# Attention layer of an encoder trunk: ScalarE in written order in the q, k, v stage, and VectorE in place of accumulating DMAs in the output projection

## The chip, the cores and the metric

The kernel runs on one core of a Trainium2 chip. The metric is the device time of one execution in microseconds, as the median of several executions. The engines of the core have names in the profile: PE is TensorE (matmuls; PEld its weight loads), DVE is VectorE, ACT is ScalarE, POOL is GpSimd and SP is SyncE, which issues most of the DMAs.

## The reference

Two layers over two sequences of 512 tokens with 1024 features: a Fourier mixer with its MLP, then grouped-query attention with its MLP. All values are fp32. The change lies in the attention layer:

```python
def gqa_attention(h, w_qkv, q_gain, k_gain, w_o):
    B, S, _ = h.shape
    qkv = h @ w_qkv
    ...
    q = rms_norm(q, q_gain)
    k = rms_norm(k, k_gain)
    ang_row, ang_col = axial_angles(S)
    q = axial_rope(q, ang_row, ang_col) * (HEAD_DIM ** -0.5)
    k = axial_rope(k, ang_row, ang_col)
    ...
        s = jnp.einsum("bqkgd,bskd->bkgqs", q_blk, k)
        p = jax.nn.softmax(s, axis=-1)
        return jnp.einsum("bkgqs,bskd->bqkgd", p.astype(v.dtype), v)
    ...
    return o @ w_o

def trunk(...):
    for i in range(DEPTH):
        ...
            x = x + gqa_attention(rms_norm(x, attn_norm[j]), ...)
        x = x + sq_relu_mlp(rms_norm(x, mlp_norm[i]), mlp_w_up[i], mlp_w_down[i])
    return rms_norm(x, final_norm)
```

There are 8 heads of 128 features and 2 key and value heads, so 16 heads in all over both sequences.

## The kernel before

**Numbers.** Every fp32 operand is split into a high and a low half in a rounded format: ScalarE casts the high half (`split`, L85) and VectorE subtracts it for the low one (L86). A product is three matmuls (`mm3`, L80 to L82; `product`, L835). The large products with weights use sums of blocks in the manner of Strassen and Winograd, so that four blocks need seven products; `Blocks` makes these sums of the activations, and the weights' own sums come from `keep` and other helpers.

**Stages around the change.** `second_product(0)` ends the first MLP; its adds of PSUM into the result are L1039, its last ones with the common part L1179 and L1180. Then come three column groups, `cg` = 2 (k and v), 0 and 1 (q), in that order; for each group two sequences, and for each of these four tiles of 128 tokens. One tile is 24 matmuls into one of eight PSUM banks (`qkv`). ScalarE copies the tile to SBUF with the token's scale (L1506, L1511), squares each head with a sum (`head_squares`, L1325), and `norm_rope` takes the root (L134 to L140: VectorE, with the square root L135 on ScalarE), scales the heads by it (ScalarE, L1343), and rotates (VectorE L1348 and L1351, GpSimd L1353). `norm_rope` is a generator: its first part runs with its own tile, the rest one tile later. In between a step of `keep` is taken, which loads rows of the weight `w_o`, forms their block sums on VectorE (L1441), splits them (L1459) and stores them in DRAM (`kept`).

**The transition.** The last two tiles of q are worked in among the first heads. Between them stand head 0's scores (`scores`: maximum L1385 on VectorE, exponential L1387 on ScalarE, reciprocal L1388, scaling L1389 on GpSimd) and head 1's transposed q (`transpose_q`: L1374 on TensorE, then a split).

**Heads.** In step n TensorE does, four times over, a block of scores of head n and four transposes of the probabilities of head n−1 (L1395), then L1374 for head n+1 and the 12 matmuls of the values of head n−1 (`values`). In steps 6, 8, 10 and 12 `load_kept` (L1551) loads one of the first rows of `w_o` and splits it in two halves.

**Output projection** (from L1554). Its seven products are turned over four row blocks `m`: first b11 and b21, which give the first sequence's first half, then t2, t3, t4, then t1 and b22. The product of b11 plus that of t2 is a common part `e[m]`, to which three of the four result blocks add. `add` (L1561) is VectorE's add of a PSUM bank, and `common` (L1565) starts DMAs on GpSimd's queue that add `e[m]` to a block of the result. Each finished block is squared (`square`: L160 on ScalarE, sums L164 on GpSimd, or left apart for the last), multiplied by its gain (L206) and stored (`put_away`). The squares are summed over features by L172 on TensorE; from these come the root and its spread over the tokens (L180), and with them the operands of the second MLP (L219 norm, L235 `first_lo`).

**What sets the order.** Each engine runs its own queue in order. The order of a queue is mostly made by a scheduler at build time; within `manual_schedule` an engine's instructions stand in the order in which the code is written. Buffers come from pools: `u` (activations), `t` (temporaries), `w` (weights), `raw` (landed weights) and `ps` (the eight PSUM banks).

Of the kernel before, what the change touches and what calls it, by code (L numbers as in the profile page):

```python
# [18 lines left out]
P = 128  # L19
# [24 lines left out]
def trunk_kernel(ctx, tc, x_in, xt_in, y_out, dcos, dsin, feat, rope, gfour, gcol, grow, gfin,  # L44
# [1276 lines left out]

    def head_squares(raw, h0, n, ss):
        junk = tm((P, n * HD), BF16)
        for h in range(h0, h0 + n):
            nc.scalar.activation(junk[:, (h - h0) * HD : (h - h0 + 1) * HD], raw[:, h * HD : (h + 1) * HD],  # L1325
                                 AF.Square, accum_out=ss[:, h : h + 1])

    def norm_rope(raw, nh, table, ts, outs, ss=None, step=None, eng=nc.vector):

        n = nh * len(ts)  # L1330
        step = nh if step is None else step
        if ss is None:
            ss = small(n)
            head_squares(raw, 0, n, ss)
        r = small(n)
        rsqrt(r[:, :n], ss[:, :n], n, 1.0 / HD)
        yield
        for h0 in range(0, n, step):
            t = ts[h0 // nh]
            t1, t2 = [tm((P, step, HD)) for _ in range(2)]  # L1340
            x = raw[:, h0 * HD : (h0 + step) * HD].rearrange("p (h d) -> p h d", h=step)
            for i in range(step):
                nc.scalar.activation(x[:, i], x[:, i], AF.Copy, scale=r[:, h0 + i : h0 + i + 1])  # L1343
# [118 lines left out]
    def load_kept():  # L1462

        i = len(ahead)
        if i < 4:
            w = load_w(w_o[i, 0], nc.vector, 2)
        elif i in (8, 9):
            w = load_w(w_a22[i - 8])
        else:
# [4 lines left out]
            w = t[:, 0], t[:, 1]  # L1474
        ahead.append([(w[0][:, i : i + 512], w[1][:, i : i + 512]) for i in (0, 512)])

# [5 lines left out]
    keeping, turned = keep(), iter(())  # L1482
    for cg in (2, 0, 1):
        ws = wkv if cg == 2 else [load_w(w_qkv[cg, u], home=own if u < 2 else lent) for u in range(4)]
        for q in range(NSEQ):
            if cg == 2:
                vt[q] = (slot([P, NT, 256], F32R), slot([P, NT, 256], F32R))
                kr[q] = slot([P, NT, 256], F32)
            else:
                for i in range(2):  # L1490
                    qr[q, 2 * cg + i] = slot([P, NT, 256], F32)
            for t in range(NT if (cg, q) != (1, 1) else 2):
                if (cg, q, t) in transposes:
                    transpose_k(transposes[cg, q, t])
                if (cg, q, t) == (1, 1, 1):
                    first = transpose_q(0, 0)
                if (cg, q) == (2, 0):
                    o = qkv(cg, q, t, ws, KC - 2, KC, begun[t])
                else:
                    o = qkv(cg, q, t, ws)  # L1500
                if (cg, q, t) == (2, 0, 0):
                    token_scale(1)
                r = rs[q][:, t : t + 1]
                if cg == 2:
                    raw = tm((P, 256))
                    nc.scalar.activation(raw, o[:, :256], AF.Copy, scale=r)  # L1506
                    split_scaled(vt[q][0][:, t], vt[q][1][:, t], o[:, 256:], r)
                    todo = norm_rope(raw, NKV, rt["k"], [t], [kr[q][:, t]])
                else:
                    raw = slot([P, 512], F32) if (cg, q, t) == (1, 1, 1) else tm()  # L1510
                    nc.scalar.activation(raw, o, AF.Copy, scale=r)  # L1511
                    todo = norm_rope(raw, 4, rt["q"], [t], [qr[q, 2 * cg + i][:, t] for i in range(2)])
                next(todo)
                for _ in turned:
                    pass
                turned = todo
                if cg != 2 or q or t:
                    next(keeping, None)


    heads = [(q, h) for q in range(NSEQ) for h in range(NH)]
    raw, ss = slot([P, 1024], F32), small(8)
    o = qkv(1, 1, 2, ws)
    probs = [scores(*heads[0], first, t) for t in range(NT)]
    nc.scalar.activation(raw[:, :512], o, AF.Copy, scale=rs[1][:, 2:3])
    head_squares(raw, 0, 4, ss)
    qT = transpose_q(*heads[1])
    for _ in turned:
        pass
    o = qkv(1, 1, 3, ws)  # L1530
    nc.scalar.activation(raw[:, 512:], o, AF.Copy, scale=rs[1][:, 3:4])
    todo = norm_rope(raw, 4, rt["q"], [2, 3], [qr[1, 2 + i][:, t] for t in (2, 3) for i in range(2)],
                     ss, 2, nc.gpsimd)
    assert next(keeping, 0) == 0
    for n in range(1, len(heads) + 1):
        pts, nxt = [], []
# [23 lines left out]
    def add(x, o):  # L1560
        nc.vector.tensor_add(x, o, x)  # L1561

    def common(m, *xs):
        for x in xs:
            nc.gpsimd.dma_start(x, e[m], accum_op=ALU.add)  # L1565

# [8 lines left out]
    with tc.manual_schedule(engines={ET.PE}):  # L1575
        o = {}
        for m, i in turn():
# [3 lines left out]
            if i:  # L1581
                add(xs[0, m][:, 0], o[m])
                load_kept()
            else:
                nc.scalar.copy(e[m], o[m])
            if m + i > 1:
                next(todo)
        load_xs(1, park[1])
        for k, name in enumerate(("t2", "t3", "t4")):
            h = heads_out.operand(name)  # L1590
            for m in range(4):
                o = ps()
                product(o, ahead[4 + 2 * k + m // 2][m % 2], h)
# [8 lines left out]
                if k == 2:  # L1602
                    blocks.gain(0, 2 * m)
                    blocks.gain(0, 2 * m + 1)
                    put_away(0, m)
                if m % 2:
                    load_kept()
                next(todo, None)
        o = {}
        for j, (m, i) in enumerate(turn()):  # L1610
# [13 lines left out]
            if 1 < j < 6:  # L1624
                blocks.first(j - 2)
            if 2 < j < 7:
                blocks.first_lo(j - 3)
    second_product(1, blocks, ())
    ats = []
# [269 lines left out]
```

## Time and profile before

| | |
|---|---|
| median of 3 runs | 1716.38 us (1715.95 to 1716.51) |
| the profiled execution | 1714.8 us |
| its span, first to last instruction | 1713.0 us |
| mean granted TensorE clock | 0.994 |
| q, k, v stage, transition, heads, projection | from about 740, 850, 870, 992 us of the span |

In the page's first part stand each engine's busy time, its share of the span and its number of instructions. A row of a timeline has the start in us from the span's begin, the duration, the engine, the line, the operation, its buffers (out<-in), its shape and the number of instructions that were joined to one row; behind it in brackets how long the engine had been idle and what ended this. A row of groups has busy time, the mean in ns of one instruction and the idle time before them with what ended it. A row of windows has the length, then PE, PEld, DVE, ACT and POOL with busy time and count, then the granted clock, the busy share of the DMA engines and GB/s.

### The profile page before, as it was taken

The numbers are of one execution on the slowest core, as the hardware profiler recorded it, in microseconds if no ns is written. First come the engines' busy times: TensorE is split into PE (matmuls) and PEld (weight loads), VectorE is DVE, ScalarE is ACT, GpSimd is POOL, SyncE is SP. The second block draws the span as 40 slices with busy tenths as digits, with TensorE's granted clock in tenths as the row PEclk, the third lists the DMA queues.
The fourth block names the chain that finished last, engine by engine and source line by source line (L and its number), as shares of the span: only waits on it lengthen the run. The fifth ranks groups of instructions, "written<-read, shape, count | busy, mean of one in ns | idle before, by whom it ended". The sixth has DMA issues, their size and how long they took to land.

```text
span 1713.0 us, 22359 instructions
## 1 busy us (share of the span) xinstructions
PE 1666.6 (97%) x7826; PEld 1386.3 (81%) x7826; DVE 1260.9 (74%) x1880; ACT 885.6 (52%) x1568; POOL 384.1 (22%) x360
## 2 busy tenths in 40 slices
PE   5999999999999999999989999999999999999998
PEld 4988888888888888788868887788788888888887
DVE  8769777546886869977678773787855577878875
ACT  6766445446342434456788753564444563433334
POOL 1320443231000001333344323102432220000002
PEclk9999999999999999999999999999999999999999
DMA  8652555449864757435400158334543596756622
GB/s 276 164 206 98 189 186 185 166 168 339 292 221 154 244 179 224 158 139 181 142 25 1 50 179 239 141 110 156 201 168 142 199 373 212 240 157 218 186 105 99
DMA packets 123394, 304.54 MB, mean 178 GB/s; under 512 B 12537, under 2 KB 13689, under 8 KB 123281
## 3 DMA queue, kind: packets, MB, share of 16 engines
q1 hardware_dynamic: 99040, 254.61, 42.1%
q0 software_dynamic: 9984, 22.55, 6.6%
q10 hardware_dynamic: 14256, 25.96, 4.0%
q8 instruction: 61, 1.00, 0.2%
q14 instruction: 53, 0.43, 0.1%
HBM read 216.49 MB, written 82.38 MB: 174 GB/s over the span
## 4 chain that ended last, share of the span: by engine, by line
PE 42%; DVE 4%; ACT 3%; DMA 1%; issue 1%; POOL 0%; DVEq 0%; ACTq 0%; POOLq 0%
PE ps L835 34%; PE ps L81 2%; PE ps L82 2%; PE ps L80 2%; PE ps L1395 1%; DMA raw<-w_sum 1%; DVE u L86 1%; ACT t L1325 1%; DMA u<-t 0%; ACT t L1387 0%; ACT t L1343 0%; ACT u L85 0%; DVE w L86 0%; PE ps L172 0%; PE ps L1374 0%
## 5 line engine op out<-in xcount | busy, mean ns | idle before, releaser
L835 PE MATMUL ps<-u,w 128*128 128x512 f32 x4992 | 1145.2, 390 | 5.0 <-DVE w L86 2.9
L835 PEld LDWEIGHTS ps<-u,w 128*128 128x128 f32 x4992 | 936.6, 188 | 204.3 <-DVE w L86 4.7
L85 ACT CAST w<-raw 128x1024 fp32r<-128x1024 f32 (+1 forms) x226 | 220.2, 981 | 318.3 <-PE ps L835 244.8
L86 DVE TENSOR_TENSOR w<-raw,w 128x1024 fp32r<-128x1024 f32 (+1 forms) x226 | 262.5, 1166 | 82.5 <-ACT w L85 82.2
L85 ACT CAST u<-u 128x1024 fp32r<-128x1024 f32 x144 | 144.6, 1047 | 82.2 <-PE ps L835 38.9
L86 DVE TENSOR_TENSOR u<-u,u 128x1024 fp32r<-128x1024 f32 x144 | 173.3, 1231 | 16.2 <-ACT u L85 15.8
L80 PE MATMUL ps<-u,u 128*128 128x512 f32 (+2 forms) x360 | 137.1, 383 | 7.0 <-ACT u L85 3.7
L1039 DVE TENSOR_TENSOR u<-ps,u 128x512 f32<-128x512 f32 x160 | 109.3, 684 | 36.6 <-PE ps L835 34.0
L949 POOL TENSOR_TENSOR u<-u 128x512 f32<-128x512 f32 x28 | 37.7, 1347 | 430.4 <-ACT u L848 430.4
L835 PE MATMUL ps<-u,u 128*128 128x512 f32 x552 | 132.2, 390 | 2.0 <-DVE t L918 2.0
L1068 POOL DMA_DIRECT2D raw<-w_sum x32 | 27.9, 871 | 471.2 <-DMA raw<-w_sum 158.7
L82 PE MATMUL ps<-u,u 128*128 128x512 f32 (+2 forms) x360 | 132.4, 368 | 1.0 <-DVE u L86 0.6
L81 PE MATMUL ps<-u,u 128*128 128x512 f32 (+2 forms) x360 | 131.6, 366 | 0.3 <-DVE u L86 0.3
L835 PEld LDWEIGHTS ps<-u,u 128*128 128x128 f32 x552 | 103.4, 188 | 24.5 <-issue 2.8
L164 POOL TENSOR_TENSOR t<-t,t 128x512 f32<-128x512 f32 (+1 forms) x52 | 76.8, 1481 | 169.5 <-ACT t L160 168.8
L847 ACT ACTIVATE t<-t 128x512 f32<-128x512 f32 x64 | 40.4, 632 | 114.1 <-DVE t L918 104.3
L80 PEld LDWEIGHTS ps<-u,u 128*128 128x128 f32 x360 | 69.8, 194 | 17.5 <-ACT u L85 4.4
L82 PEld LDWEIGHTS ps<-u,u 128*128 128x128 f32 x360 | 69.6, 193 | 12.5 <-DVE u L86 1.6
L81 PEld LDWEIGHTS ps<-u,u 128*128 128x128 f32 x360 | 70.0, 194 | 8.8 <-DVE u L86 0.9
L86 DVE TENSOR_TENSOR u<-ps,u 128x512 fp32r<-128x512 f32 (+4 forms) x118 | 70.7, 623 | 8.1 <-ACT u L85 7.7
L907 DVE TENSOR_TENSOR t<-ps,u 128x512 f32<-128x512 f32 x32 | 22.0, 687 | 62.0 <-PE ps L835 58.3
L160 ACT ACTIVATE t<-u 128x512 f32<-128x512 f32 (+1 forms) x64 | 37.8, 603 | 56.9 <-DVE u L1561 29.9
(236 smaller groups left out, 1993.0 us busy)
## 6 DMA issues: line engine op xcount, KB each, us to landing
raw<-w_up SPq DMA_DIRECT2D x80, 512.0 KB, 4.5
u<-spill_t SPq DMA_DIRECT2D x60, 512.0 KB, 7.1
raw<-w_sum SPq DMA_DIRECT2D x56, 512.0 KB, 5.3
u<-spill_b SPq DMA_DIRECT2D x45, 512.0 KB, 6.3
spill_t<-u SPq DMA_DIRECT2D x84, 256.0 KB, 2.0
spill_b<-t ACTq DMA_DIRECT2D x60, 256.0 KB, 4.2
raw<-w_row SPq DMA_DIRECT2D x28, 512.0 KB, 4.4
park<-u SPq DMA_DIRECT2D x24, 512.0 KB, 4.3
```

The costliest lines, as they stand in the source:

```text
L80: nc.tensor.matmul(out, lh, rh, start=first, stop=False)
L81: nc.tensor.matmul(out, lh, rl, start=False, stop=False)
L82: nc.tensor.matmul(out, ll, rh, start=False, stop=last)
L85: nc.scalar.copy(dst_hi, src)
L86: eng.tensor_sub(dst_lo, src, f32(dst_hi))
L160: nc.scalar.activation(s[:, :n], xt(q, fo)[:, :n], AF.Square)
L164: nc.gpsimd.tensor_add(acc[q][:, :n], acc[q][:, :n], s[:, :n])
L835: nc.tensor.matmul(o, w[x][:, sl], h[k][y], start=first and k + i == 0, stop=k == n - 1 and i == 2, skip_group_check=not first)
L847: nc.scalar.activation(t, src, AF.Relu)
L949: eng.tensor_sub(t[:, 0], b12, b11)
L1039: nc.vector.tensor_add(x, o, x)
L1068: nc.gpsimd.dma_start(s[:, 1], w[:, 3], accum_op=ALU.add)
```

## The change

It has three parts.

*q, k, v.* `tile_qkv` no longer copies a tile out of PSUM. The squares read the PSUM bank with the token's scale r, the root is multiplied by r (one small VectorE operation more per tile), and the scaling before the rotation reads PSUM too and writes a temporary; the bank is held until the next tile. Only the last three tiles are still copied. ScalarE's instructions stand in written order in the three groups and in the transition. The weights of the next group are loaded and split one per tile (`next_ws`), and `keep` starts at the second sequence of group 2.

*First rows.* `load_kept` is a generator: in steps 7 and later of the heads' loop it loads a first row of `w_o` into an activation buffer and splits one half per step, in steps 8 to 15. Before, the scheduler had drawn these splits forward into the q, k, v stage and the transition (w<-raw of 128x512 there).

*Output projection.* `common` is gone. At t2 VectorE adds the bank to `e[m]` and `e[m]` to the first sequence's second half; at t3 it adds the bank and then `e[m]` to both halves of the second sequence in one instruction 1024 wide; t4 accumulates in the PSUM bank of t3. The squares of the first sequence's even blocks move from t3 to t2, and their gains from t4 to t3. `first_lo` of blocks 2 and 3 is written after the loop.

```diff
-    def norm_rope(raw, nh, table, ts, outs, ss=None, step=None, eng=nc.vector):
+    def norm_rope(raw, nh, table, ts, outs, ss=None, step=None, eng=nc.vector, scale=None):
...
-            head_squares(raw, 0, n, ss)
+            head_squares(raw, 0, n, ss, 1.0 if scale is None else scale)
+            yield
         r = small(n)
         rsqrt(r[:, :n], ss[:, :n], n, 1.0 / HD)
+        if scale is not None:
+            nc.vector.tensor_scalar(r[:, :n], r[:, :n], scale, 1.0, ALU.mult, ALU.mult)
         yield
...
-            x = raw[:, h0 * HD : (h0 + step) * HD].rearrange("p (h d) -> p h d", h=step)
+            y = raw[:, h0 * HD : (h0 + step) * HD].rearrange("p (h d) -> p h d", h=step)
+            x = y if scale is None else tm((P, step, HD))
             for i in range(step):
-                nc.scalar.activation(x[:, i], x[:, i], AF.Copy, scale=r[:, h0 + i : h0 + i + 1])
+                nc.scalar.activation(x[:, i], y[:, i], AF.Copy, scale=r[:, h0 + i : h0 + i + 1])
...
-            w = load_w(w_o[i, 0], nc.vector, 2)
+            raw, w = slot([P, 1024], F32), own()
+            nc.sync.dma_start(raw, w_o[i, 0])
...
+        for j in range(2 if i < 4 else 0):
+            yield
+            split(*ahead[i][j], raw[:, j * 512 : j * 512 + 512])
...
+    def tile_qkv(cg, q, t):
...
+        r = rs[q][:, t : t + 1]
+        if cg == 2:
+            split_scaled(vt[q][0][:, t], vt[q][1][:, t], o[:, 256:], r)
+            return norm_rope(o, NKV, rt["k"], [t], [kr[q][:, t]], scale=r)
+        outs = [qr[q, 2 * cg + i][:, t] for i in range(2)]
+        if (cg, q, t) != (1, 1, 1):
+            return norm_rope(o, 4, rt["q"], [t], outs, scale=r)
+        raw = slot([P, 512], F32)
+        nc.scalar.activation(raw, o, AF.Copy, scale=r)
+        return norm_rope(raw, 4, rt["q"], [t], outs)
...
+    with tc.manual_schedule(engines={ET.Activation}):
+        for cg in (2, 0, 1):
+            later = next_ws({2: 0, 0: 1}[cg]) if cg != 1 else iter(())
...
+                    todo = tile_qkv(cg, q, t)
+                    next(todo)
+                    for _ in turned:
+                        pass
+                    if q or t > 1 or cg == 0:
+                        next(later, None)
+                    for _ in range(cg != 2 or q):
+                        next(keeping, None)
+                    next(todo)
+                    turned = todo
...
-        if n in (6, 8, 10, 12):
-            load_kept()
+        if n > 6:
+            next(first_rows, None)
...
-    def common(m, *xs):
-        for x in xs:
-            nc.gpsimd.dma_start(x, e[m], accum_op=ALU.add)
...
-                if k < 2:
-                    add(e[m], o)
-                    common(m, *((xs[1, m][:, 0],), (xs[0, m][:, 1], xs[1, m][:, 1]))[k])
+                    o[m] = ps()
+                product(o[m], ahead[4 + 2 * k + m // 2][m % 2], h, k < 2)
+                if k == 0:
+                    add(e[m], o[m])
+                    square(0, 2 * m)
+                    add(xs[0, m][:, 1], e[m])
+                elif k == 1:
+                    add(xs[1, m][:, 1], o[m])
+                    add(xs[1, m], e[m].unsqueeze(1).broadcast_to([P, 2, 512]))
+                    blocks.gain(0, 2 * m)
                 else:
-                    add(xs[0, m][:, 1], o)
-                if k:
-                    fo = 2 * m + k - 1
-                    square(0, fo, alone=fo == KC - 1)
...
+                    add(xs[0, m][:, 1], o[m])
+                    square(0, 2 * m + 1, alone=m == 3)
```

How the rows stand now. ScalarE at the transition, before: the tile (1,1,1) of q is copied (L1511), squared and scaled (L1343), tile (1,1,2) copied (L1525); then the exponentials' table and head 0's exponentials (L1387), and the cast of head 1's transposed q (L85).

```order
L1511 ACTIVATE u_7623<-ps_7598,rs_6317 128x512
L1325 ACTIVATE t_7626,s_7625<-u_7623 128x128 x4
L135 ACTIVATE s_7634<-s_7632 128x4
L1343 ACTIVATE u_7623<-u_7623,s_7631 128x128 x4
L1525 ACTIVATE u_7654<-ps_7656,rs_6317 128x512
L1387 ACT_TABLE_LOAD
L1387 ACTIVATE t_7688,s_7686<-ps_7681,s_7685 128x512
L1387 ACTIVATE t_7699,s_7697<-ps_7692,s_7696 128x512
L85 CAST u_7736<-ps_7731 128x512
```

The same place with the change (lines moved by 5 and more: L1528 and L1563 are the copies, L1348 the scaling, L1392 the exponentials):

```order
L1528 ACTIVATE u_7624<-ps_7599,rs_6319 128x512
L1325 ACTIVATE t_7627,s_7626<-u_7624 128x128 x4
L1348 ACTIVATE t_7634<-ps_7530,s_7578 128x128 x4
L135 ACTIVATE s_7647<-s_7645 128x4
L1392 ACT_TABLE_LOAD
L1392 ACTIVATE t_7693,s_7691<-ps_7686,s_7690 128x512
L1392 ACTIVATE t_7704,s_7702<-ps_7697,s_7701 128x512
L1392 ACTIVATE t_7715,s_7713<-ps_7708,s_7712 128x512
L1392 ACTIVATE t_7726,s_7724<-ps_7719,s_7723 128x512
L1563 ACTIVATE u_7657<-ps_7661,rs_6319 128x512
L85 CAST u_7736<-ps_7731 128x512
```

Between squares and root of tile (1,1,1) now stands the scaling of the tile before it (t_7634 from PSUM); its own scaling has gone behind the cast, and four exponentials instead of two stand ahead of the cast.

VectorE in the projection from t3 on, before (t_9394 to t_9397 are `e`, u_9398 to u_9404 the first sequence's blocks, u_9559 one of the second's):

```order
L86 TENSOR_TENSOR u_9673<-u_9345,u_9672 128x1024
L1561 TENSOR_TENSOR t_9395<-ps_9676,t_9395 128x512
L1561 TENSOR_TENSOR t_9396<-ps_9698,t_9396 128x512
L1561 TENSOR_TENSOR t_9397<-ps_9717,t_9397 128x512
L1561 TENSOR_TENSOR u_9398<-ps_9739,u_9398 128x512
L1561 TENSOR_TENSOR u_9400<-ps_9760,u_9400 128x512
L1561 TENSOR_TENSOR u_9402<-ps_9784,u_9402 128x512
```

With the change (L1599 is `add`; t_9400 to t_9403 are `e`, u_9565 to u_9571 the second sequence, u_9404 the first):

```order
L86 TENSOR_TENSOR u_9689<-u_9349,u_9688 128x1024
L1599 TENSOR_TENSOR u_9565<-t_9400,u_9565 128x1024
L1599 TENSOR_TENSOR u_9567<-ps_9692,u_9567 128x512
L1599 TENSOR_TENSOR u_9569<-ps_9712,u_9569 128x512
L1599 TENSOR_TENSOR u_9567<-t_9401,u_9567 128x1024
L1599 TENSOR_TENSOR u_9569<-t_9402,u_9569 128x1024
L1599 TENSOR_TENSOR u_9571<-ps_9729,u_9571 128x512
L1599 TENSOR_TENSOR u_9571<-t_9403,u_9571 128x1024
L1599 TENSOR_TENSOR u_9404<-ps_9671,u_9404 128x512
```

The adds of a bank to `e` at t3 have become adds to the second sequence, and behind each stands an add of `e`, 1024 wide, with both inputs in SBUF.

VectorE at the end of the first MLP, before: the adds of `keep` (L1441) stand among those of the product (L1039).

```order
L1180 TENSOR_TENSOR u_4162<-u_4162,t_3889 128x1024
L1039 TENSOR_TENSOR u_3824<-ps_5997,u_3824 128x512
L1441 TENSOR_TENSOR raw_6386<-raw_6386 128x512
L90 SCALAR_TENSOR_TENSOR u_5961<-u_4044,gc,u_5961 128x512
L1179 TENSOR_TENSOR u_3824<-u_3824,t_3889 128x512
L1039 TENSOR_TENSOR u_4277<-ps_6094,u_4277 128x512
L1441 TENSOR_TENSOR raw_6386<-raw_6386,raw_6387 128x512
L1441 TENSOR_TENSOR raw_6592<-raw_6592,raw_6591 128x512
L1441 TENSOR_TENSOR raw_6387<-raw_6387,raw_6386 128x512
L1039 TENSOR_TENSOR u_4277<-ps_6108,u_4277 128x512
```

With the change:

```order
L1180 TENSOR_TENSOR u_4162<-u_4162,t_3889 128x1024
L86 TENSOR_TENSOR w_6060<-raw_5995,w_6060 128x1024
L1039 TENSOR_TENSOR u_3824<-ps_5997,u_3824 128x512
L1179 TENSOR_TENSOR u_3824<-u_3824,t_3889 128x512
L90 SCALAR_TENSOR_TENSOR u_5961<-u_4044,gc,u_5961 128x512
L1039 TENSOR_TENSOR u_4277<-ps_6094,u_4277 128x512
L1039 TENSOR_TENSOR u_4277<-ps_6108,u_4277 128x512
```

The adds of `keep` are gone from there, and L1180 stands ahead of a weight's split (L86), which it followed before.

More of the change, by code (lines that the diff above doesn't have):

```diff
@@ new lines, in trunk_kernel, with next_ws, split_ws @@
+    ws = {2: wkv}
+    def next_ws(cg):
+        ws[cg], raw = [], []
+        for u in range(4):
+            raw.append(load_raw(w_qkv[cg, u]))
+            if u:
+                yield
+                split_ws(cg, raw[u - 1])
+        yield
+        split_ws(cg, raw[3])
+        yield
+    def split_ws(cg, raw):
+        w = (own if len(ws[cg]) < 2 else lent)()
+        split(*w, raw)
+        ws[cg].append(w)
+    def tile_qkv(cg, q, t):
+        if (cg, q, t) in transposes:
+            transpose_k(transposes[cg, q, t])
+        if (cg, q) == (2, 0):
+            o = qkv(cg, q, t, ws[cg], KC - 2, KC, begun[t])
+        else:
+            o = qkv(cg, q, t, ws[cg])
+        if (cg, q, t) == (2, 0, 0):
+            token_scale(1)
+        r = rs[q][:, t : t + 1]
[8 more added lines that the diff above has]
+        return norm_rope(raw, 4, rt["q"], [t], outs)
@@ L1521, in trunk_kernel @@
     heads = [(q, h) for q in range(NSEQ) for h in range(NH)]
     raw, ss = slot([P, 1024], F32), small(8)
[L1523 to L1531, printed above, removed]
+    with tc.manual_schedule(engines={ET.Activation}):
+        o = qkv(1, 1, 2, ws[1])
+        probs = [scores(*heads[0], first, t) for t in range(NT)]
+        nc.scalar.activation(raw[:, :512], o, AF.Copy, scale=rs[1][:, 2:3])
+        qT = transpose_q(*heads[1])
+        for _ in turned:
+            pass
+        o = qkv(1, 1, 3, ws[1])
+        nc.scalar.activation(raw[:, 512:], o, AF.Copy, scale=rs[1][:, 3:4])
+        head_squares(raw, 0, 4, ss)
@@ L1625, in trunk_kernel @@
                 blocks.first(j - 2)
-            if 2 < j < 7:
+            if 2 < j < 5:
                 blocks.first_lo(j - 3)
+        for i in range(2, 4):
+            blocks.first_lo(i)
     second_product(1, blocks, ())
```

64 lines of the change are left out of this document (19 added, 45 removed).

## The prediction

> **What bounds the kernel now.** First the page's busy times, then TensorE's timeline at every place where it idles, then what ScalarE (ACT) and VectorE (DVE) did just before. All sums are against the profiled execution, 1714.8 us (span 1713.0 and 1.8 around it); the median shown, 1716.4, is 1.6 above it.
>
> ```profile
> PE 1666.6 (97%) x7826; PEld 1386.3 (81%) x7826; DVE 1260.9 (74%) x1880; ACT 885.6 (52%) x1568; POOL 384.1 (22%) x360
> ```
>
> TensorE (PE) is busy for 97%: the matmuls, which the change leaves as they are, are the bound. What can be won is idle time and half-clock time after it. Four such places lie near the edit. The transition from projection to heads, TensorE's timeline (start, us, what, idle before):
>
> ```profile
> 854.12 0.60 PE L1374 MATMUL ps<-ident,u 128*128 128x128 f32 x4
> 854.47 0.49 PE L80 MATMUL ps<-w,u 128*128 128x512 f32 x1
> ...
> 859.83 0.39 PE L82 MATMUL ps<-u,u 128*128 128x512 f32 x1
> 863.42 0.50 PE L80 MATMUL ps<-u,u 128*128 128x512 f32 x1 [3.21 <-ACT u L85]
> ...
> 867.20 0.47 PE L1395 MATMUL ps<-ident,t 128*128 128x128 f32 x1 [1.54 <-POOL t L1389]
> ...
> 872.73 0.60 PE L1374 MATMUL ps<-ident,u 128*128 128x128 f32 x4
> 880.47 0.60 PE L1374 MATMUL ps<-ident,u 128*128 128x128 f32 x4
> ```
>
> From 854.47 to 859.83 stand 24 matmuls, 0.233 apart, so work could have gone on at 860.06. A head takes 7.74 (872.73 to 880.47); less 0.35 for L1374 and 12 matmuls (2.8) the four blocks of scores and transposes are 4.6. L1374 was therefore due at 864.7 and came at 872.73: **8.0 lost**, of it 3.21 and 1.54 in waits and the rest at half clock. The windows, whose third number from the end is the granted clock before DMA share and GB/s:
>
> ```profile
> 864.60:871.40 6.80, 5.26 (x18) 3.82 (x18) 6.80 (x12) 5.66 (x18) 4.35 (x5) 0.50 0.26 82
> 1052.30:1059.20 6.90, 6.75 (x23) 5.97 (x24) 0.72 (x5) 2.20 (x6) 0.00 (x0) 0.51 0.87 308
> 1083.00:1090.00 7.00, 7.00 (x31) 5.66 (x32) 3.71 (x3) 1.92 (x4) 0.93 (x1) 1.00 0.58 195
> ```
>
> Two stretches of about 6.8 us run at 0.50, behind the two longest waits; no other stretch here does. The second is the end of the output projection's first half:
>
> ```profile
> 1050.77 0.38 PE L172 MATMUL ps<-ones,t 128*128 128x2 f32 x2 [2.02 <-POOL t L164]
> 1052.45 3.15 PE L172 MATMUL ps<-ones,t 128*128 128x2 f32 x14 [1.30 <-ACT t L160]
> 1055.46 7.46 PE L835 MATMUL ps<-u,w 128*128 128x512 f32 x24
> 1062.76 0.60 PE L180 MATMUL ps<-ident,s 128*128 128x128 f32 x4
> 1063.12 0.71 PE L835 MATMUL ps<-u,w 128*128 128x512 f32 x2
> ...
> 1099.00 0.95 PE L172 MATMUL ps<-ones,t 128*128 128x2 f32 x8
> ```
>
> TensorE had run dry at 1048.75 (1050.77 less 2.02). At full clock, eight L172 take 0.95: sixteen 1.9, the 24 matmuls 5.6, L180 0.36 (1062.76 to 1063.12), so the last row was due near 1056.5: **6.6 lost**.
>
> **The change part by part.** *Transition.* ScalarE before it, and its groups from 747 to 860 (busy, mean ns, idle before):
>
> ```profile
> 854.41 0.66 ACT L1511 ACTIVATE u<-ps,rs 128x512 f32<-128x512 f32 x1
> 858.28 1.28 ACT L1343 ACTIVATE u<-u,s 128x128 f32<-128x128 f32 x4 [1.15 <-DVE s L140]
> 859.47 0.67 ACT L1525 ACTIVATE u<-ps,rs 128x512 f32<-128x512 f32 x1
> 860.16 1.28 ACT L1387 ACT_TABLE_LOAD   x1
> 862.79 0.58 ACT L85 CAST u<-ps 128x512 fp32r<-128x512 f32 x1
> ```
> ```profile
> L1343 ACT ACTIVATE t<-t,s 128x128 f32<-128x128 f32 x68 | 23.1, 392 | 20.1 <-DVE s L140 20.0
> L1325 ACT ACTIVATE t<-t 128x128 bf16<-128x128 f32 x68 | 20.2, 300 | 0.3
> L1459 ACT CAST t<-raw 128x512 fp32r<-128x512 f32 x16 | 9.7, 609 | 0.0
> L85 ACT CAST w<-raw 128x512 fp32r<-128x512 f32 (+1 forms) x7 | 5.5, 806 | 2.2 <-DMA raw<-w_qkv 1.3 <-DMA raw<-w_o 0.9
> ```
>
> ScalarE is late there because each tile's L1343 waits 1.15 for VectorE's root; the idle sum of 20 us is this wait. Tile (1,1,1) left TensorE about 24 matmuls and a score block (8.4) before 854.1, and is copied only at 854.41. In the new order the previous tile's rotation fills the wait, the copies are gone, and the cast of head 1's q stands behind four exponentials and one copy. Scores of head 0 end on TensorE near 854.1. The last exponential then ends near 856.0 (two take 862.79 − 861.44, so 0.68 each, after VectorE's maximum of about as long), the copy adds 0.67, the cast 0.58: 857.3, the low half 0.7 later. TensorE wants it at 860.06, so 2 us to spare. GpSimd's scalings, which cost the 1.54, follow the exponentials and come earlier too. What is late next: four squares (4 × 0.30) now stand ahead of head 1's first exponential. That can cost nothing or, where nothing covers it, 1.2; I take 0.3, near nothing, since that head's probabilities are transposed a whole head later. **−7.7.**
>
> The clock's part of this is read from the windows. The Trainium skill ("TensorE: Matmul & The Clock Gate", Part 1: The HAM clock gate) has the clock halve after one idle window of about 3.4 us and return after one busy window; by that each half-clock stretch would cost 1.7, not 3.1 to 3.3, and the sum an estimated 3 less. The windows show 6.8 us each, and a drop behind 2.02 + 1.30 with matmuls between, so the measurement decides and the sum goes by the rows.
>
> *Projection.* VectorE at the stall, and GpSimd's accumulating transfers (count, min/median/max ns):
>
> ```profile
> 1037.90 0.69 DVE L1561 TENSOR_TENSOR u<-ps,u 128x512 f32<-128x512 f32 x1 [2.03 <-PE ps L835]
> ...
> 1045.62 0.69 DVE L1561 TENSOR_TENSOR u<-ps,u 128x512 f32<-128x512 f32 x1 [4.30 <-DMA u<-t]
> 1051.05 1.29 DVE L1561 TENSOR_TENSOR u<-ps,u 128x512 f32<-128x512 f32 x2 [4.74 <-DMA u<-t]
> ```
> ```profile
> L1565 POOL DMA_DIRECT2D u<-t x12: 855/872/1197, 1017.3 to 1045.8; - x12
> DMA to landing us min/median/max: 3.9/7.5/9.3
> ```
>
> The last adds wait 4.30 and 4.74 for transfers that land up to 9.3 us after issue; the squares and L172 follow. The change drops these twelve issues (12 × 0.87 of GpSimd, off the path) and gives VectorE eight more adds. Their price, same engine, 1012 to 1110:
>
> ```profile
> L235 DVE TENSOR_TENSOR u<-u,u 128x1024 fp32r<-128x1024 f32 x4 | 7.5, 1889 | 0.0
> L86 DVE TENSOR_TENSOR u<-u,u 128x1024 fp32r<-128x1024 f32 x5 | 6.0, 1217 | 0.0
> ```
>
> Four are 1024 wide, four half that: 4 × 1.22 + 4 × 0.69 = 7.6, or at most 4 × 1.89 + 4 × 0.95 = 11.4. From the end of one tile near 1013.4 to the last near 1046.1 pass 12 tiles of 2.72 (0.69 + 2.03), 32.7 us; VectorE has 12 adds (8.3), eight splits at 1.22 (9.8) and these 7.6: 25.7. The lag it builds up in t2 and t3 is given back in t4, where each tile leaves 2.03. The last add then ends at 1046.8, the last square 0.63 later (it stands alone on ScalarE), and TensorE wants it at 1048.6: no wait, no half clock. **−6.6**; at the upper price 29.5, still inside.
>
> A rule speaks against this: by the Trainium skill ("SBUF — State Buffer", Who interferes with whom) a VectorE instruction with two inputs in SBUF contends with a GpSimd instruction that reads SBUF. The trace agrees (1889 against 1217 ns for one shape); it is the upper price, and a rival below.
>
> *End of the first MLP.* TensorE, then VectorE:
>
> ```profile
> 710.39 8.00 PE L835 MATMUL ps<-u,w 128*128 128x512 f32 x34 [1.07 <-DVE w L86]
> 719.20 2.14 PE L835 MATMUL ps<-u,w 128*128 128x512 f32 x8 [0.81 <-DVE u L1039]
> ```
> ```profile
> 710.25 1.21 DVE L1180 TENSOR_TENSOR u<-u,t 128x1024 f32<-128x1024 f32 x1
> ...
> 714.46 4.09 DVE L1441 TENSOR_TENSOR raw<-raw,raw 128x512 f32<-128x512 f32 x3
> ```
>
> keep() starts later, so its three adds (4.09) no longer stand before L1039: −1.1 (0.81 and the pipeline's refill). In its place L1180 (1.21) instead of an add of 0.68 stands ahead of the split that TensorE awaits at 710.39: +0.5. **−0.6**, between −1.1 and +0.5, if the first goes by another wait.
>
> *First rows among the heads.* Eight splits of 512, one in each of heads 8 to 15, which hold none now:
>
> ```profile
> 866.28 1.14 ACT L85 CAST w<-raw 128x512 fp32r<-128x512 f32 x2
> 867.34 1.82 DVE L86 TENSOR_TENSOR w<-raw,w 128x512 fp32r<-128x512 f32 x2
> 925.00:960.00 35.00, 35.00 (x201) 29.30 (x200) 28.18 (x62) 27.69 (x66) 12.48 (x19) 1.00 0.00 1
> ```
>
> A head of 7.74 leaves ScalarE 1.6 and VectorE 1.5; a split takes 0.57 and 0.91. So between nothing and 8 × 1.48 = 11.8 (no cover at all); I take +0.4, near nothing, because both fit. **Sum: −7.7 − 6.6 − 0.6 + 0.4 = −14.5**: 1700.3 of the profiled run, 1701.9 beside the median.
>
> **Rivals.** (1) *The transition's wait only moves*: four exponentials instead of two stand before the cast; were ScalarE still 5 us behind, nothing there is won: 1709.6. Against it: the wait that made the lag is filled. (2) *VectorE bounds the projection*: with every two-input operation at the 1889 price (adds 11.4, splits 15.1, PSUM adds 8.3: 34.8 of 32.7) the last add is 2.1 late, past a slack of 1.2; with a clock drop 3.3 + 0.9 return, at worst all 6.6: 1706 to 1708.5. Against it: GpSimd has less to do there than before. (3) *The heads lose* the whole uncovered price: 1713.3. (4) **Slower**: ScalarE's written order blocks. Every cast of keep (L1459) and of weights now stands in line before the squares that release PSUM; if the data come late, all wait. A tile lasts 5.6; ScalarE needs 1.2 + 1.6 + 0.61 + 0.2 + at most 1.05, 4.7, so 0.9 is free. Over 16 tiles the transfers would have to hold it 1.8 per tile (14.5 / 16 and the 0.9) to eat the whole gain and reach 1716.4, and 2.0 to pass 0.2%, about 1720. Its casts waited 2.2 for transfers in the whole stage. (5) *first_lo moved to after the loop*: VectorE's order there is unchanged, so the stalls behind it stay; nothing in the sum rests on it.
>
> **Chances.** Forecast 0.72; (1) 0.09; (2) 0.08; (3) or a good part of it 0.05; (4) 0.03; a sum short for reasons not seen 0.03. The range goes from 1698.5 (nothing given back in the transition, the heads or the MLP's end: 1700.7; the gap of 1.6 between profile and median gone; the 0.6 over which the runs spread) to 1710, which takes in (1) and (2). Faster by over 0.2%, about what a measurement can tell from no change (below 1713): 0.92; within: 0.04; slower: 0.04.
>
> **What would show it.** Right: no clock at 0.5 between 860 and 1060 of the old time, L1374 18.6 us apart become 10.7, L172 without idle before it, no accumulating transfer, heads 8 to 15 at 7.74. Wrong: L80 waiting for ACT L85 again, VectorE's adds without idle in t4, a head at 8 or more with the weight cast ahead, TensorE idle behind ScalarE's squares between 747 and 850.

## The result and the profile after

The changed kernel takes 1707.38 us (median of 4 runs, 1705.45 to 1708.37) against 1716.16 for the kernel before in the same sessions: the ratio is 0.9948, with an interval of 0.993 to 0.9965. Of the 14.5 us that the prediction summed up, 8.8 came. The changed kernel's profiled execution was the slowest of its four (1708.37, span 1706.6), so the two profiles differ by 6.4 only. The sums below are between profiled executions.

Where the time went is read from TensorE's starts at five places that every version has: the first L172 behind the first MLP, the first transposes of q (L1374 before, L1379 after), those of head 3, those of the last head, and the add of the projection that waits 0.7 (1075.01 before, 1069.38 after). Differences of these starts, in us:

| stretch | before | after | predicted change | measured change |
|---|---|---|---|---|
| to the first L172 | 738.41 | 738.90 | −0.6 | +0.5 |
| q, k, v, to the first transposes of q | 101.61 | 101.54 | 0 | −0.1 |
| transition, to head 3's transposes | 40.45 | 39.95 | −7.7 | **−0.5** |
| heads, to the last one's transposes | 95.55 | 96.56 | +0.4 | +1.0 |
| projection, to the add that waits 0.7 | 98.99 | 92.43 | −6.6 | **−6.6** |
| rest of the span | 637.99 | 637.22 | 0 | −0.8 |

The projection did what was worked out; the transition did not. First the projection. TensorE's timeline of the changed kernel at the place where it had idled 2.02 and 1.30:

```profile
1049.85 1.84 PE L172 MATMUL ps<-ones,t 128*128 128x2 f32 x16
1051.55 5.75 PE L835 MATMUL ps<-u,w 128*128 128x512 f32 x24
1057.13 0.60 PE L180 MATMUL ps<-ident,s 128*128 128x128 f32 x4
```

No row has a wait in brackets, and the 24 matmuls take 5.75 instead of 7.46. VectorE ahead of it, from the last tiles of t3 on:

```profile
1033.61 1.28 DVE L1599 TENSOR_TENSOR u<-ps,u 128x512 f32<-128x512 f32 x2
1034.81 2.35 DVE L1599 TENSOR_TENSOR u<-t,u 128x1024 f32<-128x1024 f32 x2
1037.08 0.69 DVE L1599 TENSOR_TENSOR u<-ps,u 128x512 f32<-128x512 f32 x1
1037.80 1.23 DVE L1599 TENSOR_TENSOR u<-t,u 128x1024 f32<-128x1024 f32 x1
1039.16 0.69 DVE L1599 TENSOR_TENSOR u<-ps,u 128x512 f32<-128x512 f32 x1
1041.88 0.69 DVE L1599 TENSOR_TENSOR u<-ps,u 128x512 f32<-128x512 f32 x1 [2.03 <-PE ps L835]
```

VectorE falls behind in t3 (it is hardly idle from 1033.6 to 1039.2), and from t4's second tile on it waits 2.03 for TensorE again: the lag is given back where the prediction put it. The wide add costs 1.23 or less, the lower price.

Now the transition. TensorE's timeline of the changed kernel:

```profile
855.95 0.79 PE L80 MATMUL ps<-u,u 128*128 128x512 f32 x1 [3.98 <-ACT u L85]
...
861.54 0.72 PE L1379 MATMUL ps<-ident,u 128*128 128x128 f32 x4
...
867.96 0.50 PE L80 MATMUL ps<-u,u 128*128 128x512 f32 x1 [0.20 <-ACT u L85]
...
872.61 0.60 PE L1379 MATMUL ps<-ident,u 128*128 128x128 f32 x4
```

Before, the scores of head 1 waited 3.21 for a cast of ScalarE. Now those of **head 0** wait 3.98, for the cast of head 0's q, and the half clock follows as before (0.57 as the mean of 854.0 to 860.8). The wait at head 1 is down to 0.20. So the wait has moved one head forward. Two things in the rows make it. The first is the place of the cast in ScalarE's queue. Before, it stood ahead of the squares of tile (1,1,0); in the written order it stands behind these squares and behind the scaling and the cast of `keep` that follow them. First the row of before, then that of the changed kernel:

```profile
849.36 0.57 ACT L85 CAST u<-ps 128x512 fp32r<-128x512 f32 x1
```
```profile
855.30 0.60 ACT L85 CAST u<-ps 128x512 fp32r<-128x512 f32 x1
```

TensorE was ready for it near 852.0 (855.95 less 3.98). The second is that ScalarE as a whole is late: it takes up tile (1,1,0) 9.6 after TensorE's last matmul for it, before and after the change alike. Why it stays late stands in ScalarE's waits from 780 to 860, in three views: the kernel before, the changed kernel, and an experiment below (e3_root_first). The columns are total us, times and longest:

```profile
ACT t L1343 <- DVE s L140: 16.4, 11, 2.5
```
```profile
ACT t L1348 <- DVE s L1340: 31.5, 14, 4.4
```
```profile
ACT s L135 <- DVE s L134: 13.1, 13, 2.9
...
ACT t L1325 <- PE ps L82: 3.6, 3, 2.0
```

The wait of the scaling for VectorE's root, which the change was predicted to fill with other work, has nearly doubled (in e3 it is not among the waits). VectorE and ScalarE in one tile of the changed kernel, at the end of column group 0, show how:

```profile
829.11 0.69 DVE L1353 TENSOR_TENSOR t<-t,u 128x512 f32<-128x512 f32 x1 [1.14 <-ACT t L1348]
829.71 0.75 DVE L1356 TENSOR_TENSOR t<-t,u 128x256 f32<-128x256 f32 x2
830.38 0.69 DVE L1465 TENSOR_TENSOR raw<-raw,t 128x512 fp32r<-128x512 f32 x1
830.99 0.17 DVE L136 RECIPROCAL s<-s 128x4 f32<-128x4 f32 x1
831.19 0.49 DVE L137 TENSOR_TENSOR s<-s 128x4 f32<-128x4 f32 x1
831.72 0.66 DVE L138 TENSOR_TENSOR s<-s,s 128x4 f32<-128x4 f32 x1
...
832.82 0.23 DVE L1340 TENSOR_SCALAR s<-s,rs 128x4 f32<-128x4 f32 x1
```
```profile
833.08 1.14 ACT L1348 ACTIVATE t<-ps,s 128x128 f32<-128x128 f32 x4 [2.00 <-DVE s L1340]
...
838.24 1.14 ACT L1348 ACTIVATE t<-ps,s 128x128 f32<-128x128 f32 x4 [2.01 <-DVE s L1340]
```

It is a **loop over two engines**. The rotation (L1353) waits 1.14 for ScalarE's scaling of the tile; the root of the next tile (L136 to L1340) stands behind the rotation in VectorE's queue; and the next scaling on ScalarE waits 2.00 for that root. Once round takes 5.16 (833.08 to 838.24), whatever ScalarE has free in between. A tile on TensorE takes 24 matmuls, 5.44. So ScalarE makes up 0.28 of a lag per tile: of the 11.0 that it is behind at the last tile of group 0, 9.6 are left at tile (1,1,0).

### The profile page after: what moved, and what is told of

Its sections match the earlier page's. It is cut to its first block, busy times and chain, and to the rows that moved or that the text cites. A ratio compares the mean times of both kernels' runs of the same rounds, so it can differ in the third digit from the quotient of the medians.

```text
span 1706.6 us, 22348 instructions
## 1 busy us (share of the span) xinstructions
PE 1665.7 (98%) x7826; PEld 1384.0 (81%) x7826; DVE 1274.3 (75%) x1909; ACT 874.2 (51%) x1547; POOL 378.8 (22%) x348
## 4 chain that ended last, share of the span: by engine, by line
PE 77%; DVE 13%; ACT 4%; DMA 3%; issue 3%; POOL 0%; DVEq 0%; SPq 0%; ACTq 0%; POOLq 0%
PE ps L835 66%; PE ps L82 3%; PE ps L80 3%; PE ps L81 3%; DVE u L86 1%; DVE w L86 1%; PE ps L1400 1%; ACT u L85 1%; DMA raw<-w_sum 1%; ACT t L1392 1%; ACT t L1348 1%; DMA raw<-w_o 1%; DVE t L1356 1%; DMA u<-w_qkv 1%; DVE raw L1465 1%
## 5 line engine op out<-in xcount | busy, mean ns | idle before, releaser
L85 ACT CAST w<-raw 128x1024 fp32r<-128x1024 f32 (+1 forms) x218 | 215.6, 994 | 310.7 <-PE ps L835 241.7
L86 DVE TENSOR_TENSOR w<-raw,w 128x1024 fp32r<-128x1024 f32 (+1 forms) x218 | 257.2, 1183 | 74.3 <-ACT w L85 74.0
L86 DVE TENSOR_TENSOR u<-u,u 128x1024 fp32r<-128x1024 f32 x144 | 173.1, 1229 | 21.3 <-ACT u L85 20.7
L85 ACT CAST u<-u 128x1024 fp32r<-128x1024 f32 x144 | 144.5, 1046 | 84.7 <-PE ps L835 33.5
L80 PE MATMUL ps<-u,u 128*128 128x512 f32 (+2 forms) x360 | 137.3, 385 | 6.7 <-ACT u L85 4.7
L1039 DVE TENSOR_TENSOR u<-ps,u 128x512 f32<-128x512 f32 x160 | 109.5, 686 | 36.6 <-PE ps L835 33.8
L164 POOL TENSOR_TENSOR t<-t,t 128x512 f32<-128x512 f32 (+1 forms) x52 | 74.6, 1439 | 193.1 <-ACT t L160 192.6
L80 PEld LDWEIGHTS ps<-u,u 128*128 128x128 f32 x360 | 70.2, 195 | 18.7 <-ACT u L85 7.4
L86 DVE TENSOR_TENSOR u<-ps,u 128x512 fp32r<-128x512 f32 (+4 forms) x118 | 71.2, 624 | 10.2 <-ACT u L85 9.6
L85 ACT CAST u<-ps 128x512 fp32r<-128x512 f32 (+4 forms) x118 | 61.1, 545 | 6.8 <-PE ps L1400 3.4
```

The lines of the kernel that those rows point to most:

```text
L80: nc.tensor.matmul(out, lh, rh, start=first, stop=False)
L85: nc.scalar.copy(dst_hi, src)
L86: eng.tensor_sub(dst_lo, src, f32(dst_hi))
L164: nc.gpsimd.tensor_add(acc[q][:, :n], acc[q][:, :n], s[:, :n])
```

## The experiments

Each ran beside the kernel before on one chip, in two sessions: e1 to e4 with a median of 1715.62 for that kernel, e5 to e8 with 1716.8. Ratios are to the kernel before of the same session.

**e1_projection.** The kernel before with the change's output projection: its adds, the order of its squares and gains, and the place of `first_lo`.

```diff
-                    common(m, *((xs[1, m][:, 0],), (xs[0, m][:, 1], xs[1, m][:, 1]))[k])
+                    add(xs[0, m][:, 1], e[m])
...
+                    add(xs[1, m], e[m].unsqueeze(1).broadcast_to([P, 2, 512]))
```

> The kernel before with the change's output projection alone (VectorE's adds, no accumulating DMAs). Theory: the projection keeps all it promised, whatever the q, k, v stage does: the two waits at L172 and the half-clock stretch at 1052 vanish, 6.6 us less than before, about 1709.6; the transition keeps its 3.21 wait. Rival (VectorE bound by two-input adds): 1 to 4 less, with VectorE's adds still ending after 1047.5.

Measured: 1708.06 (1705.48 to 1710.0, 5 runs) against 1715.62, ratio 0.9958 (0.9945 to 0.997). The projection's stretch takes 92.10, 6.9 less than before. TensorE's timeline there and at the transition:

```profile
863.64 0.79 PE L80 MATMUL ps<-u,u 128*128 128x512 f32 x1 [3.91 <-ACT u L85]
```
```profile
1049.07 1.84 PE L172 MATMUL ps<-ones,t 128*128 128x2 f32 x16
1050.77 5.75 PE L835 MATMUL ps<-u,w 128*128 128x512 f32 x24
```

The transition's wait is the old one, at head 1 (3.91 here, 3.21 in the profile of before); the waits at L172 are gone. The projection's edit works alone and gives what the sum gave it. That VectorE becomes the bound there is refuted.

**e2_rest.** The changed kernel with the old projection.

```diff
-                    add(xs[0, m][:, 1], e[m])
...
+                    common(m, *((xs[1, m][:, 0],), (xs[0, m][:, 1], xs[1, m][:, 1]))[k])
```

> The changed kernel with the output projection of before: q, k, v in written order, rotation from PSUM and first rows among the heads alone. Theory (the transition's wait only moved, to head 0's q): transition 0.5 less, heads 1.0 more, end of the MLP 0.5 more, so 1715.5 to 1717.5, no gain. Rival (the parts help each other, or the profile of the changed kernel was an unlucky execution): 1711 or less.

Measured: 1714.93 (11 runs) against 1715.62, ratio 0.9994 (0.9985 to 1.0003): no gain that can be told from nothing, and a little below the expected 1715.5. Its timeline has both waits, the new one of the transition and the old one of the projection:

```profile
855.26 0.79 PE L80 MATMUL ps<-u,u 128*128 128x512 f32 x1 [4.06 <-ACT u L85]
```
```profile
1051.12 0.38 PE L172 MATMUL ps<-ones,t 128*128 128x2 f32 x2 [2.04 <-POOL t L164]
```

So, as far as the noise allows to tell, the changed kernel's gain is the projection's.

**e3_root_first.** The changed kernel with the root of a tile written ahead of the scaling and rotation of the tile before. One line moves:

```diff
                     next(todo)
+                    next(todo)
                     for _ in turned:
                         pass
...
-                    next(todo)
                     turned = todo
```

> The changed kernel with the root of a tile written ahead of the scaling and rotation of the tile before it, in the q, k, v stage alone. Theory (ScalarE's lag is a loop: its scaling waits for VectorE's root, which stands behind VectorE's rotation, which waits for ScalarE's scaling before; 5.15 us per tile against TensorE's 5.44, so a lag is never made up): the scaling no longer waits, a tile takes about 4.3, ScalarE is 3 us or less behind TensorE at tile (1,1,0) instead of 9.7, the wait of 3.98 for the cast of head 0's q is gone, 1700 to 1702. Rival (ScalarE's own line is too full with casts of weights and of keep, or waits for their transfers): the lag stays over 7, 1706 to 1708.

Measured: 1699.79 (1699.09 to 1700.54, 4 runs), ratio 0.991 (0.9897 to 0.9924), just under the expected 1700. ScalarE in two tiles of group 1, then VectorE, then TensorE at the transition:

```profile
837.14 1.12 ACT L1348 ACTIVATE t<-ps,s 128x128 f32<-128x128 f32 x4
838.14 0.63 ACT L1464 CAST t<-raw 128x512 fp32r<-128x512 f32 x1
840.73 0.37 ACT L1325 ACTIVATE t<-ps,rs 128x128 bf16<-128x128 f32 x1 [1.96 <-PE ps L82]
...
842.58 1.12 ACT L1348 ACTIVATE t<-ps,s 128x128 f32<-128x128 f32 x4
```
```profile
829.28 0.23 DVE L1340 TENSOR_SCALAR s<-s,rs 128x4 f32<-128x4 f32 x1
829.41 0.69 DVE L1353 TENSOR_TENSOR t<-t,u 128x512 f32<-128x512 f32 x1
```
```profile
854.56 0.60 PE L1379 MATMUL ps<-ident,u 128*128 128x128 f32 x4
865.03 0.60 PE L1379 MATMUL ps<-ident,u 128*128 128x128 f32 x4
872.79 0.60 PE L1379 MATMUL ps<-ident,u 128*128 128x128 f32 x4
```

The scaling waits for nothing, and the squares wait for TensorE (1.96): ScalarE has caught up. From head 1's transposes to head 2's pass 10.47 us (18.61 before, 11.07 in the changed kernel behind its wait), near the 10.6 that the prediction's rows give (864.7 less 854.12). The transition as a whole takes 32.32, 8.1 less than before.

**e4_no_keep_adds.** The changed kernel without the adds and subtractions of `keep`; they are sixteen, which the expectation miscounts. It stores plain rows of `w_o`, so its output is another one; it serves for the time alone.

```diff
             def add(out, a, b, op=ALU.subtract):
-                nc.vector.tensor_tensor(out=f32(out), in0=f32(a), in1=f32(b), op=op)
+                pass
```

> The changed kernel without keep's twelve pairs of adds and subtractions on VectorE (L1446), so that the stored rows of w_o are the plain ones and the output differs. Theory (these adds, ahead of rotation and root in VectorE's queue and waiting for transfers, start the lag in the second column group; the loop keeps it): scalings no longer wait 4.0, 4.4 and 3.6 there, lag at tile (1,1,0) 3 or less, 1700 to 1702.5. Rival (the lag comes from the loop or from ScalarE's casts alone): lag over 7, 1706 to 1708.

Measured: 1701.1 (4 runs), ratio 0.9916 (0.9903 to 0.993); the transition takes 32.32 here too. The loop is still there (its scalings start 5.15 apart in group 1), but the lag in groups 0 and 1 is 1.4 or less throughout, against up to 11.0. Where the lag starts in the changed kernel, VectorE and ScalarE in column group 0:

```profile
785.91 0.69 DVE L1446 TENSOR_TENSOR raw<-raw,raw 128x512 f32<-128x512 f32 x1 [2.19 <-DMA raw<-w_o]
```
```profile
793.53 1.14 ACT L1348 ACTIVATE t<-ps,s 128x128 f32<-128x128 f32 x4 [4.01 <-DVE s L1340]
```

An add of `keep` waits 2.19 for its transfer at the head of VectorE's queue, ahead of rotation and root. This scaling starts 9.78 after the one before it, against TensorE's 5.44.

**e7_scheduler_order.** The changed kernel with ScalarE left to the scheduler.

```diff
-    with tc.manual_schedule(engines={ET.Activation}):
+    if True:
```

(at both places)

> The changed kernel with ScalarE left to the scheduler in the q, k, v stage and the transition (neither part in written order). Theory (the loop of scaling, rotation and root sets the lag, in whatever order ScalarE's other work stands): period 5.15 per tile in column group 1 and lag at tile (1,1,0) over 7 again; what the transition waits for is another cast, and it loses 5 to 8; 1705 to 1709. Rival (the written order holds ScalarE up): lag under 4, 1700 to 1703.

Measured: 1709.95 (5 runs), ratio 0.9964 (0.9951 to 0.9977). The scalings stand 5.15 apart in group 1 as expected, and the time is in the expected range, but the lag is 2.9 and not over 7. The rival's lag (under 4) came, its time did not. TensorE's timeline:

```profile
761.87 0.33 PE L1369 MATMUL ps<-ident,u 128*128 128x128 f32 x1 [0.77 <-POOL u L1358]
765.21 1.33 PE L1369 MATMUL ps<-ident,u 128*128 128x128 f32 x5 [3.00 <-DVE s L137]
```

TensorE itself was held up at the transposes of k; the q, k, v stretch takes 108.41 instead of 101.54, 6.9 more. ScalarE came late to the k tiles there, and its queue shows one reason: the scheduler had put a cast of the next weights ahead of the stage's first root, that of the tokens' scale.

```profile
744.01 1.05 ACT L85 CAST w<-raw 128x1024 fp32r<-128x1024 f32 x1 [11.92 <-DMA raw<-w_qkv]
```

In the changed kernel this root's first step on ScalarE ran at 740.08, here at 746.42. (Before the change such a cast waited 9.23 and TensorE lost nothing, so this need not be the whole reason.) A later TensorE leaves ScalarE less far behind, but the order in group 0 differs as well, so how much of the smaller lag comes from the hold-up is not shown. The transition still takes 36.49, and not for another cast, as expected: TensorE waits 0.65 and 0.76 for GpSimd's scalings of head 0's probabilities (L1394), with 3.4 at half clock. Head 0 waits for nothing here, as before the change. So the written order does two things: against the scheduler's it saves the q, k, v stretch this hold-up, and it puts the cast of head 0's q late.

**e8_keep_loads_early.** The changed kernel, `keep` loading one step earlier.

```diff
             put(1, x2)
+            if m < 3:
+                r = load_parts(m + 1)
             yield
             put(3, y2)
-            if m < 3:
-                r = load_parts(m + 1)
```

> The changed kernel with keep's next two rows loaded one step earlier. Theory (the adds' own time on VectorE starts the lag, their waits for transfers, 2.2, 1.0 and 0.7 in the changed kernel, are the smaller part): lag at tile (1,1,0) falls from 9.6 to 6 to 9. Rival (the transfers are the whole cause): lag under 3, 1700 to 1702. Third (the earlier loads take the buffers of the next column group's weights): lag over 10.

Its single run took 1706.92, which decides little by itself; the trace says more. The lag is 6.9 and the transition takes 37.12, 2.8 less than in the changed kernel. So the transfers' waits are a part of the lag. That they are the smaller part, as the theory had it, is not shown: of the 3.9 that VectorE waits for `keep`'s transfers in the changed kernel (2.19, 1.02 and 0.70) 2.0 are left here (1.10 and 0.86), and the half that is gone took 2.7 of the 9.6 away.

The lag of ScalarE and the transition in all versions, from the starts of their profiled executions (lag: from the end of tile (1,1,0)'s last matmul to its first square):

| version | scalings apart in group 1 | lag at tile (1,1,0) | transition |
|---|---|---|---|
| before | 4.95 to 6.27 | 9.6 | 40.45 |
| changed | 5.13 to 5.39 | 9.6 | 39.95 |
| e2 (old projection) | 5.12 to 5.19 | 9.7 | 39.81 |
| e8 (loads early) | 5.15 to 5.20 | 6.9 | 37.12 |
| e7 (scheduler) | 5.15 to 5.40 | 2.9, TensorE held up before | 36.49 |
| e3 (root first) | 4.09, then TensorE's pace | 0.1 | 32.32 |
| e4 (no adds) | 5.14 to 5.20 | 0.1 | 32.32 |

At one written order of ScalarE's work (changed, e2, e8 and e4; e3 moves only the root) the transition falls with the lag.

**e5_first_rows_before.** e3 with the first rows of `w_o` as before the change.

```diff
-        if n > 6:
-            next(first_rows, None)
+        if n in (6, 8, 10, 12):
+            load_kept()
```

(and `load_kept` with the old load and split)

> e3_root_first with the first rows of w_o loaded and split as before the change (in the q, k, v stage, not among the heads). Theory (the heads lose 1.0 because both halves of a row are split in one head, which is 0.3 to 0.4 too full): L1379 of head 3 to that of the last goes from 96.6 back to 95.6; the eight casts now lie in ScalarE's column group 1, where e3 leaves a lag of 0 to 3, which may rise by 2; 1698 to 1700. Rival (the heads' 1.0 has another cause): 96.6 stays, 1699.5 to 1701.

Measured: 1697.75 (1696.77 to 1699.19, 4 runs), ratio 0.9898 (0.9883 to 0.9912), just under the expected 1698: **the fastest version, ahead of both kernels**. The interval overlaps that of e3, which ran in the other session, so its lead over e3 is shown by the stretch and not by the time: the heads take 95.52, as before the change. The lag at tile (1,1,0) is 0.6, with a peak of 6.6 earlier in group 1 that e3's loop has time to make up.

**e6_low_halves_gpsimd.** e3 with the low halves of these rows on GpSimd.

```diff
-            split(*ahead[i][j], raw[:, j * 512 : j * 512 + 512])
+            split(*ahead[i][j], raw[:, j * 512 : j * 512 + 512], nc.gpsimd)
```

> e3_root_first with the low halves of the first rows of w_o subtracted on GpSimd instead of VectorE. Theory (ScalarE's two casts in one head, ahead of the probabilities' casts, are what TensorE waits for): heads stay within 0.3 of 96.6, 1699.5 to 1700.5. Rival (VectorE's two subtractions are): 95.6 to 96.0, 1699. Third (GpSimd's scaling of probabilities comes late): over 97.5, 1701 or more.

Measured: 1700.01 (4 runs), ratio 0.9913 (0.9896 to 0.993). The heads take 97.46, which lies in none of the three expected ranges. In e3 the splits of three rows fall in heads that take 8.04, 8.10 and 8.10 (the fourth row's fall in the last step). Here the second and third of these take 7.89, against 7.74 without splits, so VectorE's subtractions are the larger part of the cost (0.21 of 0.36); but the first takes 9.40, since GpSimd does two subtractions (2.52) in a row ahead of a scaling:

```profile
921.63 2.52 POOL L86 TENSOR_TENSOR w<-u,w 128x512 fp32r<-128x512 f32 x2
```
```profile
924.88 0.33 PE L1400 MATMUL ps<-ident,t 128*128 128x128 f32 x1 [1.45 <-POOL t L1394]
```

## Why the prediction was right in part

The direction and the range hold, the sum does not: the time lies in the range because the range took in the rival that the transition's wait only moves, and of the sum only the projection came as worked out. Two of the prediction's own signs of being wrong came: L80 waits for ACT L85 again, and heads with the cast of a weight take 8 or more.

**Projection: right in mechanism and size.** Predicted −6.6, measured −6.6 in the changed kernel and −6.9 alone (e1). VectorE's lag in t3 and its recovery in t4 are in the trace. The rule of the Trainium skill ("SBUF — State Buffer", Who interferes with whom) that spoke against the edit had nothing to act on: GpSimd runs nothing between its sums L164 at 1016.23 (1.28) and 1040.72, and so the adds cost 0.69 and 1.23.

**Transition: the step that failed** is the sentence "In the new order the previous tile's rotation fills the wait, the copies are gone, and the cast of head 1's q stands behind four exponentials and one copy". The second half held: that cast costs TensorE 0.20. The first half did not. It looked at ScalarE's order alone. The root that the scaling waits for is VectorE's work, and VectorE's queue put it behind the rotation that waits for ScalarE. The wait rose from 16.4 to 31.5, and the lag at tile (1,1,0) stayed at 9.6. The rival that named the outcome, "the transition's wait only moves", had a chance of 0.09 and a price of 1709.6; the changed kernel came 2.2 below this price. The rows for it were at hand: the groups of before showed 20.1 of idle ahead of the scaling, and the prediction took the end of that wait for granted without laying out the period of one tile on both engines.

That the 7.7 were there to be had was right: with the loop cut (e3) the transition takes 8.1 less than before, and the kernel 1699.8, near the 1701.9 forecast for the change itself. The wait at head 0's q was not in the prediction at all: it followed the queue of ScalarE only from head 1 on, and did not see that the written order puts the cast of head 0's q behind work of the lagging tiles (855.30 against 849.36).

**Heads: a term of the right kind, undersized.** +0.4 predicted, +1.0 measured. e5 shows the cause to be these rows: without their loads and splits there the heads take 95.52. The prediction spread one split over each of eight heads; the scheduler put both halves into one, so three heads are 0.3 to 0.4 longer and the fourth row's splits fall behind them. ScalarE's casts there in the changed kernel:

```profile
931.31 0.65 ACT L85 CAST w<-u 128x512 fp32r<-128x512 f32 x1
...
932.50 0.65 ACT L85 CAST w<-u 128x512 fp32r<-128x512 f32 x1
```

**End of the first MLP: open.** −0.6 was predicted, +0.5 measured. The wait at L1039 is gone and the one at the weight's split has grown (1.07 to 1.88), as predicted, but to this came a stretch at half clock:

```profile
711.60:715.00 3.40, 3.40 (x9) 2.63 (x9) 1.99 (x4) 2.19 (x4) 2.50 (x2) 0.50 0.95 266
```

The stretch costs 1.7 at half clock. It isn't in every execution: e3 waits 1.90 at the same place and runs on at full clock. Over the versions with the same code there the first L172 starts between 735.4 and 738.9, so 1.1 of difference can't be settled from one execution each.

**first_lo: right.** The waits of 0.74 and 1.64 behind it are as they were.

**Slower by ScalarE's written order: refuted** in the sense of the rival: from 738 to 860 its casts of `keep` and of weights wait 1.6 in all, not 1.8 per tile. That the order would wait on VectorE instead was not foreseen. Two numbers of this rival were off: a tile takes 5.44 and not 5.6, and the 2.2 of waits of ScalarE's casts before the change leaves out one of 9.23 for `w_qkv` at 742.69, just ahead of the stretch that was read; e7 has the same wait (11.92).

## What to carry to other kernels

Where two engines hand a tile back and forth, lay the period of one tile out on both queues before moving work on one of them: an engine that idles behind another's result is not helped by fuller order on its own side. A loop whose period is just under the bound's (5.16 against 5.44 here) hides in steady state and gives a lag back only slowly (0.28 per tile); look for what starts the lag (an add that waits for a transfer at the head of a queue) and for the step that can leave the loop (the root, which needed nothing from the rotation it stood behind). Check the first place where a lagging engine is waited for, not only the place where the old profile shows the wait.

## What the runs showed of the hardware

VectorE's smallest operations are not of one length. In the loop above L137 and L138 take 0.49 and 0.66 while GpSimd adds (L1358, 830.56 to 832.36); in e3 they stand where GpSimd's add ends and take 0.20 and 0.17, while L134, which there runs beside the add, takes 0.70 instead of 0.16. In the loop the two make 0.8 of the 5.16, an estimate from these rows. L137 and L138 have two inputs in SBUF and fit the rule that the prediction quotes from the Trainium skill ("SBUF — State Buffer", Who interferes with whom); L134 has one, and that rule does not cover it. That the loop would be shorter without GpSimd's add was not tried.

The clock: behind the 1.88 wait at 710.37 the half-clock stretch was 3.40 long, half of the 6.8 at the other places, and behind a wait of 1.90 in e3 there was none:

```profile
711.80:715.20 3.40, 3.40 (x15) 2.82 (x16) 3.19 (x5) 2.04 (x4) 1.27 (x2) 1.00 0.91 296
```

So one idle time of about 2 us may cost nothing or 1.7 here. In e2 a wait of 2.04 at L172, with one of 0.21 behind it, was followed by 6.8 at half clock, while 1.91 at 711.25 of the same trace was followed by none. In all traces of this case the stretches at half clock, but for the one at each span's end, are 3.4, 6.8 or 10.2 long, the last in e1 behind waits of 3.91 and 1.43. What decides between these lengths is not shown.
